# A hybrid S5 / attention / gated-MLP layer on one core: another order of the seven products in the up projection, single PSUM banks in the down projection, and VectorE for the late low parts

## The chip, the cores and the metric

The kernel runs on 1 core of one Trainium2 chip, as one program. The metric is the device time of one execution in microseconds (us), the median of several runs. A profile is one further execution, recorded by the hardware profiler; its span runs from the first to the last instruction.

## The reference

One layer of a diffusion backbone works on 1,024 latent tokens of 1,024 channels, with 256 context tokens beside them. Its first half mixes tokens (a state-space branch and differential attention); the change leaves it alone. Its second half is a gated MLP with a short convolution, and all of the change lies there:

```python
def conv_ffn(h, w_up, conv_w, conv_b, w_down):
    u = h @ w_up
    n = u.shape[1]
    pad = CONV_W // 2
    up = jnp.pad(u, ((0, 0), (pad, pad), (0, 0)))
    y = conv_b
    for j in range(CONV_W):
        y = y + up[:, j:j + n] * conv_w[j]
    a, g = jnp.split(y, 2, axis=-1)
    return (jax.nn.silu(g) * a) @ w_down
...
    x = x + ga1 * merge_branches(g, y_s5, y_attn, p['b_gate'], p['w_out'])
    x = x + ga2 * conv_ffn(modulate(x, p['norm2_w'], sh2, sc2), p['w_up'], p['conv_w'], p['conv_b'], p['w_down'])
```

D_FF is 2816 = 22 x 128, so `w_up` has 44 blocks of 128 columns: 22 for `a` and 22 for `g`.

## The kernel before

**Data.** Activations lie transposed: 128 channels on the partitions, 1,024 tokens along the free axis, in two halves `t0` and `t1` of 512. Each operand of a matmul is split in a high part (`copy` to fp32r, by ScalarE) and a low part (source minus high part, by VectorE or GpSimd); a product is high x high, high x low and low x high, three matmuls for each block of 128 input channels. One PSUM bank holds 128 x 512 fp32 values.

**The up projection** makes, for each hidden block f of 22, the two tiles `va` (the `a` rows) and `ga` (the `g` rows), 128 x 1,024 each, in two banks each. Weights (two blocks of output rows, two halves `lo` and `hi` of the input channels) and activations (two halves of the channels, two halves of the tokens) make a 2 x 2 by 2 x 2 block product, done with seven products instead of eight (Winograd's form of Strassen's algorithm). The activations' factors, `B11`, `B21`, `T1`, `T2`, `B22`, `T3`, `T4`, are made once, at the *seam* before f = 0, by `modulate0` and `modulate1`; `factor` makes high and low part of one block. The weights' factors are made for each f: `up_open` splits the `a` weights, `sums` makes S1 to S4 by four additions, and `piece` splits each. The gate's raw half `A22` is a factor as it is.

For each f, `up_open` runs two products of 12 matmuls: `lo` x B11 into a single bank (`bank()`, 2 buffers `z`), copied out as p1, and `hi` x B21 into `va`'s lower half (`banks()`, 3 buffers `up` of two banks). `up_close` runs the other five products: S1 x T1 (upper half of `ga`), S2 x T2, S4 x B22 (upper half of `va`), S3 x T3 (single bank) and A22 x T4 (lower half of `ga`), with VectorE's sums between them. The sums are u2 (product S2 x T2 plus p1), p1 again (upper `ga` plus u2), u3 (product S3 x T3 plus u2), and one that completes each half of `va` and `ga`. Then `gated` convolves both tiles (`conv`: one pass by ScalarE, four by VectorE, straight from PSUM), applies SiLU and multiplies; the result goes to memory (`Fd`) until the down projection.

**The down projection** sums over the 22 hidden blocks in five parts. For each part and each output block m of 8, both halves of the tokens have a gemm of 3 x (blocks of the part) matmuls into a bank, and VectorE adds the bank, scaled, to `x1[m]` (L1664). For even m the two halves take two single banks `z`, for odd m one tile `up` of two banks. `parted` splits the hidden blocks, by VectorE for the first part and by GpSimd for the rest; GpSimd also makes the low parts of all `w_down` blocks.

**Order.** TensorE's instructions stand as the program writes them (`manual_schedule`). The queues of VectorE, ScalarE, GpSimd and the DMA queue of SyncE are ordered when the program is built, by a scheduler; each engine runs its queue in order and waits on semaphores. Waits are set by whole tiles: an instruction that writes one half of a tile waits for all earlier readers and writers of that tile on other engines.

## Time and profile before

| | before |
|---|---|
| median of 3 runs | 2249.25 us (2249.17 to 2251.09) |
| the profiled execution, its own time | 2250.89 us |
| its span | 2249.1 us |
| mean granted clock of TensorE | 0.961 of full |
| TensorE matmul busy | 2061.7 us, 92% of the span |
| VectorE busy | 1358.4 us, 60% |
| GpSimd busy | 926.4 us, 41% |
| ScalarE busy | 843.4 us, 37% |
| first product of the up projection | 1399.90 us after the start |
| first matmul of the down projection | 1973.23 us |

Engines are named PE (TensorE), DVE (VectorE), ACT (ScalarE), POOL (GpSimd) and SP (SyncE). The granted clock is the share of TensorE's full 2.4 GHz that the chip let through; its two levels are 1.2 and 2.4 GHz, so a mean between 0.5 and 1 is a mixture of both. The stretch from 1399.90 us to the end, 849.2 us, holds everything that the change touches.

### The profile page before, as it was taken

The numbers are of one execution on the slowest core, as the hardware profiler recorded it, in microseconds if no ns is written. First come the engines' busy times: TensorE is split into PE (matmuls) and PEld (weight loads), VectorE is DVE, ScalarE is ACT, GpSimd is POOL, SyncE is SP. The second block draws the span as 40 slices with busy tenths as digits, with TensorE's granted clock in tenths as the row PEclk, the third lists the DMA queues.
The fourth block names the chain that finished last, engine by engine and source line by source line (L and its number), as shares of the span: only waits on it lengthen the run. The fifth ranks groups of instructions, "written<-read, shape, count | busy, mean of one in ns | idle before, by whom it ended". The sixth has DMA issues, their size and how long they took to land.

```text
span 2249.1 us, 29026 instructions
## 1 busy us (share of the span) xinstructions
PE 2061.7 (92%) x10392; PEld 1667.0 (74%) x10392; DVE 1358.4 (60%) x2606; ACT 843.4 (37%) x1509; POOL 926.4 (41%) x1016
## 2 busy tenths in 40 slices
PE   7988899989999999999999999588888888889998
PEld 4766688756688879999998777466777677667776
DVE  6988924999830428888885525765555555542211
ACT  4334434122123227888884023433333333331110
POOL 2476401344104513666665556443333333264311
PEclk9999999999999999999999999799899999999999
DMA  8345654455664263223212554022121121343212
GB/s 308 115 103 143 160 172 145 143 156 149 217 219 155 89 220 109 80 85 104 75 50 67 168 182 127 28 94 66 57 69 68 61 66 66 114 141 108 56 46 88
DMA packets 164625, 262.49 MB, mean 117 GB/s; under 512 B 28672, under 2 KB 92544, under 8 KB 164480
## 3 DMA queue, kind: packets, MB, share of 16 engines
q1 hardware_dynamic: 154400, 242.28, 35.1%
q10 hardware_dynamic: 10080, 18.35, 2.2%
q8 instruction: 82, 1.34, 0.3%
q14 instruction: 63, 0.52, 0.1%
HBM read 188.68 MB, written 71.89 MB: 116 GB/s over the span
## 4 chain that ended last, share of the span: by engine, by line
PE 67%; DVE 23%; DMA 4%; issue 3%; ACT 2%; POOL 2%; SPq 0%; DVEq 0%; ACTq 0%; POOLq 0%
PE ta L1040 6%; PE up L1488 4%; PE up L1489 4%; PE up L1490 4%; PE sc L1240 3%; PE sc L1241 3%; PE up L1267 3%; PE z L1269 3%; PE z L1268 3%; PE z L1267 3%; PE up L1268 3%; PE up L1269 3%; DVE y L1685 2%; PE tb L1022 2%; PE z L555 2%
## 5 line engine op out<-in xcount | busy, mean ns | idle before, releaser
L1242 DVE TENSOR_REDUCE mx<-sc 128x1 f32<-128x1280 f32 x128 | 190.8, 1491 | 53.2 <-PE sc L1241 52.3
L597 POOL TENSOR_TENSOR wlo<-wraw,whi 128x1024 fp32r<-128x1024 f32 x40 | 97.6, 2456 | 245.6 <-ACT whi L596 243.6
L418 PE MATMUL z<-whi,hTh 128*128 128x512 f32 x448 | 182.4, 411 | 3.6 <-ACT hTh L407 3.6
L419 PE MATMUL z<-wlo,hTh 128*128 128x512 f32 x448 | 181.2, 405 | 0.3 <-POOL wlo L597 0.3
L420 PE MATMUL z<-whi,hTl 128*128 128x512 f32 x448 | 179.5, 402 | 0.0
L995 ACT ACTIVATE e<-sc,mx 128x1280 f32<-128x1280 f32 x128 | 172.0, 1344 | 12.6 <-DVE mx L1242 10.9
L1040 PE MATMUL ta<-V,at 128*128 128x128 f32 x1280 | 168.1, 275 | 0.7 <-ACT at L1029 0.7
L1040 PEld LDWEIGHTS ta<-V,at 128*128 128x128 f32 x1280 | 155.5, 191 | 1.0 <-ACT at L1029 0.9
L1488 PE MATMUL up<-tt,rh 128*128 128x512 f32 x176 | 88.0, 500 | 74.4 <-DVE up L1556 74.4
L1685 DVE SCALAR_TENSOR_TENSOR y<-up,small,y 128x896 f32<-128x896 f32 (+1 forms) x176 | 123.7, 745 | 53.3 <-ACT y L1680 52.5
L1240 PE MATMUL sc<-K,q 128*128 128x512 f32 (+1 forms) x384 | 147.7, 385 | 0.7 <-ACT e L995 0.7
L1241 PE MATMUL sc<-K,q 128*128 128x512 f32 (+1 forms) x384 | 131.9, 358 | 0.0
L1481 POOL TENSOR_TENSOR pl<-s,ph 128x512 fp32r<-128x512 f32 x44 | 58.8, 1339 | 174.9 <-ACT ph L1480 174.9
L1255 POOL TENSOR_TENSOR wlo<-wraw,whi 128x1024 fp32r<-128x1024 f32 (+1 forms) x36 | 74.9, 2084 | 120.9 <-ACT whi L1254 120.9
L1659 POOL TENSOR_TENSOR wlo<-wraw,whi 128x640 fp32r<-128x640 f32 (+2 forms) x40 | 56.1, 1404 | 161.8 <-ACT whi L1658 160.8
L1488 PEld LDWEIGHTS up<-tt,rh 128*128 128x128 f32 x176 | 42.2, 240 | 93.5 <-DVE up L1556 72.7
L418 PEld LDWEIGHTS z<-whi,hTh 128*128 128x128 f32 x448 | 86.5, 193 | 33.4 <-issue 10.6
L555 PE MATMUL z<-hTh,whi 128*128 128x512 f32 x256 | 102.4, 400 | 0.0
L420 PEld LDWEIGHTS z<-whi,hTl 128*128 128x128 f32 x448 | 86.9, 194 | 19.3 <-issue 1.0
L557 PE MATMUL z<-hTh,wlo 128*128 128x512 f32 x256 | 100.6, 394 | 0.0
L556 PE MATMUL z<-hTl,whi 128*128 128x512 f32 x256 | 100.2, 393 | 0.0
L1013 DVE SCALAR_TENSOR_TENSOR e<-e,r,e 128x1280 f32<-128x1280 f32 x64 | 99.3, 1552 | 1.1
(497 smaller groups left out, 5736.2 us busy)
## 6 DMA issues: line engine op xcount, KB each, us to landing
wraw<-in_wup_dram SPq DMA_DIRECT2D x46, 512.0 KB
wraw<-in_win_dram SPq DMA_DIRECT2D x44, 512.0 KB
araw<-in_ada_dram SPq DMA_DIRECT2D x32, 512.0 KB
q<-Qd SPq DMA_DIRECT2D x128, 128.0 KB
Kd<-st SPq DMA_DIRECT2D x80, 128.0 KB
K<-Kd SPq DMA_DIRECT2D x16, 640.0 KB
Fd<-y SPq DMA_DIRECT2D x20, 512.0 KB
graw<-Fd SPq DMA_DIRECT2D x20, 512.0 KB
```

Of the source, the lines that this page charges most:

```text
L418: nc.tensor.matmul(pz, hh, wh, start=k == 0, stop=False)
L419: nc.tensor.matmul(pz, hh, wl, start=False, stop=False)
L420: nc.tensor.matmul(pz, hl, wh, start=False, stop=k == KT - 1)
L555: nc.tensor.matmul(pz, wh, hTh[k][:, tok], start=k == 0, stop=False)
L995: nc.scalar.activation(em, S[i]["sc"][m][:, :LK], AF.Exp, bias=S[i]["mx"][:, m:m + 1], accum_out=S[i]["l1"] if m else S[i]["l0"])
L1040: nc.tensor.matmul(PO[p][:, j * P:j * P + P], AT[p, kt // 2][:, kt % 2, j * P:j * P + P], W[:, kt], start=kt == 0, stop=kt == NKT - 1)
L1240: nc.tensor.matmul(sc[:, a:b], Q[0][:, m, qs], K[m][:, a:b], start=True, stop=False)
L1241: nc.tensor.matmul(sc[:, a:b], Q[1][:, m, qs], K[m][:, a:b], start=False, stop=True)
L1242: nc.vector.tensor_reduce(S["mx"][:, m:m + 1], sc[:, :LK], axis=AX.X, op=OP.max, negate=True)
L1267: mm(o, W[0][:, k], ah[k], start=k == 0, stop=False)
L1488: mm(o, W[0][:, k], bh[k], start=k == 0, stop=False)
L1685: stt(y[:, o], pu[:, i], ww, y[:, o], op0=OP.mult, op1=OP.add)
```

## The change

The five products of `up_close` stand in another order, A22 x T4 ahead of S3 x T3. The two sums that end `ga` become one over both halves, with u3 broadcast. To go with that, `sums` and `up_close` make the pieces in the order S4, A22, S3, and `modulate1` makes T4 ahead of T3. All low parts of `factor` are VectorE's, where GpSimd made every second one of T1 and T2, and for f = 0 VectorE makes the low parts of the three late pieces. The down projection gets a PSUM pool of its own, `psD`, with eight single banks, opened once the last block's convolution is issued; that `gated` call now stands ahead of the splits of the first two blocks.

```diff
--- before.py
+++ after.py
@@ -1420,12 +1420,12 @@
             spare += [w[:, 0], w[:, 1]]
         spare = iter(spare)
 
-        def factor(name, k, src, e):
+        def factor(name, k, src):
             if k == 0:
                 B[name] = ([], [])
             h, l = next(spare), next(spare)
             nc.scalar.copy(h, src)
-            e.tensor_tensor(l, src, r32(h), op=OP.subtract)
+            nc.vector.tensor_tensor(l, src, r32(h), op=OP.subtract)
             B[name][0].append(h)
             B[name][1].append(l)
 
@@ -1456,29 +1456,28 @@
             pz = spread(1)
             tt = nc.vector.tensor_tensor
             t0, t1 = halves
-            v, g = nc.vector, nc.gpsimd
             for k in range(KH):
                 b12 = scaled(k, 1, pz)
                 tt(x1[k][:, t0], b12, x1[k][:, t0], op=OP.subtract)
-                factor("T1", k, x1[k][:, t0], v if k % 2 else g)
+                factor("T1", k, x1[k][:, t0])
             for k in range(KH):
                 b22 = scaled(k + KH, 1, pz)
                 tt(x1[k][:, t0], b22, x1[k][:, t0], op=OP.subtract)
-                factor("T2", k, x1[k][:, t0], v if k % 2 else g)
+                factor("T2", k, x1[k][:, t0])
             for k in range(KH):
-                factor("B22", k, x1[k + KH][:, t1], v)
+                factor("B22", k, x1[k + KH][:, t1])
+            for k in range(KH):
+                tt(x1[k + KH][:, t0], x1[k + KH][:, t0], x1[k][:, t0], op=OP.subtract)
+                factor("T4", k, x1[k + KH][:, t0])
+            for k in range(KH):
                 tt(x1[k][:, t1], x1[k + KH][:, t1], x1[k][:, t1], op=OP.subtract)
-                tt(x1[k + KH][:, t0], x1[k + KH][:, t0], x1[k][:, t0], op=OP.subtract)
-            for k in range(KH):
-                factor("T3", k, x1[k][:, t1], v)
-            for k in range(KH):
-                factor("T4", k, x1[k + KH][:, t0], v)
-
-        def piece(pool, src, tag, bufs):
+                factor("T3", k, x1[k][:, t1])
+
+        def piece(pool, src, tag, bufs, e=nc.gpsimd):
             h = self.t(pool, [P, KH, P], tag + "h", bufs, F32R)
             l = self.t(pool, [P, KH, P], tag + "l", bufs, F32R)
             nc.scalar.copy(h, src)
-            nc.gpsimd.tensor_tensor(l, src, r32(h), op=OP.subtract)
+            e.tensor_tensor(l, src, r32(h), op=OP.subtract)
             return h, l
 
         def product(o, W, name):
@@ -1531,14 +1530,14 @@
             tt(a, ra[:, hi], b, op=OP.subtract)
             b = s()
             tt(b, ra[:, lo], rg[:, lo], op=OP.subtract)
-            S["rest"] = a, b, rg[:, hi]
+            S["rest"] = a, rg[:, hi], b
 
         def up_close(fp, f):
 
             p1, va = opened.pop(f)
             t0, t1 = halves
             tt = nc.vector.tensor_tensor
-            S["S4"], S["S3"], S["A22"] = (piece(fp, x, "r", 3) for x in S["rest"])
+            S["S4"], S["A22"], S["S3"] = (piece(fp, x, "r", 3, nc.gpsimd if f else nc.vector) for x in S["rest"])
             tt(va[:, t0], va[:, t0], p1, op=OP.add)
             ga = banks()
             product(ga[:, t1], S["S1"], "T1")
@@ -1549,13 +1548,13 @@
             tt(p1, ga[:, t1], u2, op=OP.add)
             product(va[:, t1], S["S4"], "B22")
             tt(va[:, t1], va[:, t1], p1, op=OP.add)
+            product(ga[:, t0], S["A22"], "T4")
             pz = bank()
             product(pz, S["S3"], "T3")
             u3 = self.t(fp, [P, 512], "q3", 1)
             tt(u3, pz, u2, op=OP.add)
-            tt(ga[:, t1], ga[:, t1], u3, op=OP.add)
-            product(ga[:, t0], S["A22"], "T4")
-            tt(ga[:, t0], ga[:, t0], u3, op=OP.add)
+            g2 = ga.rearrange("p (h n) -> p h n", h=2)
+            tt(g2, g2, u3[:, None].to_broadcast([P, 2, 512]), op=OP.add)
             return va, ga
 
         def gated(fp, f, va, ga):
@@ -1637,10 +1636,12 @@
                 e.tensor_tensor(l, g, r32(h), op=OP.subtract)
                 return h, l
 
+            raws[NF - 1] = gated(fp, NF - 1, *rows)
+            ps_st.close()
+            pd_, pd_st = self.pool("psD", space=PSUM)
             pre = {f: parted(f, nc.vector) for f in (0, 1)}
             for k in range(KT):
                 nc.sync.dma_start(x1[k], X1d[k])
-            raws[NF - 1] = gated(fp, NF - 1, *rows)
             for part, fs in enumerate(parts):
                 last = part == len(parts) - 1
                 gts = [pre[f] if f in pre else parted(f, nc.gpsimd if part else nc.vector) for f in fs]
@@ -1657,9 +1658,8 @@
                     W = [self.t(self.fw, [P, KT, P], x, 3, F32R)[:, :n] for x in ("whi", "wlo")]
                     nc.scalar.copy(W[0], rw)
                     nc.gpsimd.tensor_tensor(W[1], rw, r32(W[0]), op=OP.subtract)
-                    pu = banks() if m % 2 else None
                     for tok in halves:
-                        pd = bank() if pu is None else pu[:, tok]
+                        pd = self.t(pd_, [P, 512], "d", 8)
                         self.gemm(pd, W, [x[0][:, tok] for x in gts], [x[1][:, tok] for x in gts])
                         nc.vector.scalar_tensor_tensor(x1[m][:, tok], pd, self.modT[:, 40 + m, 0:1], x1[m][:, tok],
                                                        op0=OP.mult, op1=OP.add)
@@ -1668,7 +1668,7 @@
         dp_st.close()
         fp_st.close()
         self.fw_st.close()
-        ps_st.close()
+        pd_st.close()
 
     def conv(self, fp, pu, ft):
 
```

How the change moves instructions, at three places.

First, TensorE in the up projection, the block f = 3, as in every later one. `z` is a single bank, `up` a tile of two, `rh` and `rl` are a weight piece's two parts; before, `tt_2863` to `tt_2866` are T3 and `tt_2867` to `tt_2870` T4; a bracket names the semaphores that the instruction waits for. Before, the end of S3 x T3 and the start of A22 x T4:

```order
L1488 MATMUL z_14770<-tt_2866_13408,rh_14719 128x512
L1489 MATMUL z_14770<-tt_2866_13408,rh_14719 128x512
L1490 MATMUL z_14770<-tt_2866_13408,rl_14720 128x512
L1488 MATMUL up_14728<-tt_2867_13409,rh_14723 128x512 [waits DVE_49]
L1489 MATMUL up_14728<-tt_2867_13409,rh_14723 128x512
L1490 MATMUL up_14728<-tt_2867_13409,rl_14724 128x512 [waits Pool_49]
```

A22 x T4 is the last product and waits for VectorE. Now (`tt_2863` to `tt_2866` are T4, `tt_2867` on is T3), the end of S4 x B22 and the start of A22 x T4:

```order
L1487 MATMUL up_14667<-tt_2862_13404,rh_14712 128x512
L1488 MATMUL up_14667<-tt_2862_13404,rh_14712 128x512
L1489 MATMUL up_14667<-tt_2862_13404,rl_14713 128x512
L1487 MATMUL up_14725<-tt_2863_13405,rh_14716 128x512 [waits DVE_49,Activation_49]
L1488 MATMUL up_14725<-tt_2863_13405,rh_14716 128x512
L1489 MATMUL up_14725<-tt_2863_13405,rl_14717 128x512 [waits Pool_49]
```

A22 x T4 has moved up by one product, from behind S3 x T3 to behind S4 x B22. It still waits for VectorE: p1's sum reads the upper half of its tile. Then, in the same block, the end of A22 x T4 and the start of S3 x T3, still now:

```order
L1487 MATMUL up_14725<-tt_2866_13408,rh_14716 128x512
L1488 MATMUL up_14725<-tt_2866_13408,rh_14716 128x512
L1489 MATMUL up_14725<-tt_2866_13408,rl_14717 128x512
L1487 MATMUL z_14779<-tt_2867_13409,rh_14720 128x512 [waits Activation_49]
L1488 MATMUL z_14779<-tt_2867_13409,rh_14720 128x512
L1489 MATMUL z_14779<-tt_2867_13409,rl_14721 128x512 [waits Pool_49]
```

S3 x T3 has become the last product; it writes a single bank and waits for its piece alone.

VectorE's queue in the same block, before, from the third sum of weights to the second of `ga`'s two sums (`s` is a sum of weights, `q` are p1, u2 and u3, `y` the convolution):

```order
L1531 TENSOR_TENSOR s_14862<-wraw_14814,s_14856 128x512
L1548 TENSOR_TENSOR q_3126_14754<-z_14741,q_3108_14695 128x512
L1549 TENSOR_TENSOR q_3108_14695<-up_14728,q_3126_14754 128x512
L1533 TENSOR_TENSOR s_14864<-wraw_14814,wraw_14848 128x512
L1551 TENSOR_TENSOR up_14670<-up_14670,q_3108_14695 128x512
L1685 SCALAR_TENSOR_TENSOR y_14799<-up_14670,small_73,y_14799 128x896
L1685 SCALAR_TENSOR_TENSOR y_14799<-up_14670,small_73,y_14799 128x127
L1555 TENSOR_TENSOR q_3128_14783<-z_14770,q_3126_14754 128x512
L1685 SCALAR_TENSOR_TENSOR y_14799<-up_14670,small_73,y_14799 128x896
L1685 SCALAR_TENSOR_TENSOR y_14799<-up_14670,small_73,y_14799 128x127
L1556 TENSOR_TENSOR up_14728<-up_14728,q_3128_14783 128x512
L1558 TENSOR_TENSOR up_14728<-up_14728,q_3128_14783 128x512
```

u3 (L1555) stands between the steps of `va`'s convolution, and `ga`'s two sums are apart. VectorE's queue in that block now:

```order
L1530 TENSOR_TENSOR s_14858<-wraw_14810,s_14852 128x512
L1547 TENSOR_TENSOR q_3126_14751<-z_14738,q_3108_14692 128x512
L1548 TENSOR_TENSOR q_3108_14692<-up_14725,q_3126_14751 128x512
L1532 TENSOR_TENSOR s_14860<-wraw_14810,wraw_14844 128x512
L1550 TENSOR_TENSOR up_14667<-up_14667,q_3108_14692 128x512
L1685 SCALAR_TENSOR_TENSOR y_14795<-up_14667,small_73,y_14795 128x896
L1685 SCALAR_TENSOR_TENSOR y_14795<-up_14667,small_73,y_14795 128x127
L1685 SCALAR_TENSOR_TENSOR y_14795<-up_14667,small_73,y_14795 128x896
L1685 SCALAR_TENSOR_TENSOR y_14795<-up_14667,small_73,y_14795 128x127
L1555 TENSOR_TENSOR q_3128_14792<-z_14779,q_3126_14751 128x512
L1557 TENSOR_TENSOR up_14725<-up_14725,q_3128_14792 128x1024
```

The first five rows stand as they did. Then the convolution of `va` is no longer parted by u3, and one sum of 1,024 columns (L1557) is in the place of L1556 and L1558.

Second, the seam. GpSimd's queue before, with the four low parts of T1 and T2 (`act`) and the three late pieces of f = 0 (`rl`):

```order
L1481 TENSOR_TENSOR pl_14200<-s_14197,ph_14199 128x512
L1428 TENSOR_TENSOR act_1_1_2844_13386<-x_0_2827_13361,act_0_1_2843_13385 128x512
L1428 TENSOR_TENSOR act_5_1_2848_13390<-x_2_2829_13363,act_4_1_2847_13389 128x512
L1428 TENSOR_TENSOR act_1_1_2852_13394<-x_0_2827_13361,act_0_1_2851_13393 128x512
L1428 TENSOR_TENSOR act_5_1_2856_13398<-x_2_2829_13363,act_4_1_2855_13397 128x512
L1481 TENSOR_TENSOR rl_14295<-s_14203,rh_14294 128x512
L1481 TENSOR_TENSOR rl_14299<-s_14205,rh_14298 128x512
L1481 TENSOR_TENSOR rl_14303<-wraw_14189,rh_14302 128x512
L1481 TENSOR_TENSOR pl_14400<-s_14397,ph_14399 128x512
```

Seven of these nine are low parts for the seam.

VectorE's queue now, where the late low parts and the three pieces stand:

```order
L1428 TENSOR_TENSOR act_7_1_2858_13400<-x_3_2830_13364,act_6_1_2857_13399 128x512
L1428 TENSOR_TENSOR tt_2864_13406<-x_5_2832_13366,tt_2864_13406 128x512
L1428 TENSOR_TENSOR tt_2865_13407<-x_6_2833_13367,tt_2865_13407 128x512
L1428 TENSOR_TENSOR tt_2866_13408<-x_7_2834_13368,tt_2866_13408 128x512
L1547 TENSOR_TENSOR q_3047_14333<-z_14320,q_3008_14126 128x512
L1548 TENSOR_TENSOR q_3008_14126<-up_14307,q_3047_14333 128x512
L1480 TENSOR_TENSOR rl_14295<-s_14203,rh_14294 128x512
L1480 TENSOR_TENSOR rl_14299<-wraw_14189,rh_14298 128x512
L1480 TENSOR_TENSOR rl_14303<-s_14205,rh_14302 128x512
L1524 TENSOR_TENSOR s_14396<-wraw_14394 128x512
L1527 TENSOR_TENSOR s_14402<-s_14396,wraw_14392 128x512
L1550 TENSOR_TENSOR up_14101<-up_14101,q_3008_14126 128x512
```

None of the seven is left on GpSimd; the three `rl` stand on VectorE between p1's sum of f = 0 (L1548) and the weight sums of f = 1 (L1524), and the one that completes `va` of f = 0 (L1550) comes after those.

Third, TensorE in the down projection, where the second half of m = 1 starts. Before:

```order
L1267 MATMUL up_17622<-g_3643_17534,whi_17618 128x512
L1268 MATMUL up_17622<-g_3644_17535,whi_17618 128x512
L1269 MATMUL up_17622<-g_3643_17534,wlo_17619 128x512
L1267 MATMUL up_17622<-g_3635_17526,whi_17618 128x512 [waits DVE_49]
L1268 MATMUL up_17622<-g_3636_17527,whi_17618 128x512
L1269 MATMUL up_17622<-g_3635_17526,wlo_17619 128x512
```

The second half's first matmul waits for VectorE. The same place now:

```order
L1267 MATMUL d_17604<-g_3643_17512,whi_17600 128x512
L1268 MATMUL d_17604<-g_3644_17513,whi_17600 128x512
L1269 MATMUL d_17604<-g_3643_17512,wlo_17601 128x512
L1267 MATMUL d_17615<-g_3635_17504,whi_17600 128x512 [waits PE_49]
L1268 MATMUL d_17615<-g_3636_17505,whi_17600 128x512
L1269 MATMUL d_17615<-g_3635_17504,wlo_17601 128x512
```

Before, the second half writes the tile `up_17622` that the first half used and waits for VectorE's reading of it; now it writes another bank, `d_17615`, and waits for no other engine.

## Rows read from the trace of the kernel before

**Rows 1.** Stretches: TensorE, VectorE, ScalarE, GpSimd busy, clock, DMA.

```profile
core 0: us, PE busy (x) PEld busy (x) DVE busy (x) ACT busy (x) POOL busy (x), PEclk, DMA share, GB/s
1350.00:1399.90 49.90, 48.66 (x210) 38.69 (x210) 29.40 (x45) 18.97 (x24) 33.02 (x19) 1.00 0.43 130
1399.90:1504.71 104.81, 73.51 (x263) 55.61 (x262) 73.01 (x116) 43.32 (x63) 49.47 (x26) 0.81 0.18 62
1504.71:1973.23 468.52, 407.75 (x1597) 323.89 (x1596) 262.51 (x376) 155.18 (x190) 160.04 (x111) 0.92 0.21 71
...
1985.12:2249.10 263.98, 244.31 (x1029) 191.87 (x1027) 57.82 (x77) 42.41 (x55) 96.85 (x55) 1.00 0.29 88
```

**Rows 2.** Waits: who for whom; us in total, times, longest.

```profile
PE up L1488 <- DVE up L1556: 74.4, 22, 5.3
...
PE up L1267 <- DVE x1b L1664: 16.0, 19, 0.8
```

**Rows 3.** Timeline, TensorE, f = 3: start, length, instruction, [idle <- releaser].

```profile
1505.57 0.41 PE L1490 MATMUL z<-act,wlo 128*128 128x512 f32 x1
...
1521.51 0.40 PE L1490 MATMUL z<-tt,rl 128*128 128x512 f32 x1
1525.10 0.50 PE L1488 MATMUL up<-tt,rh 128*128 128x512 f32 x1 [3.20 <-DVE up L1556]
```

**Rows 4.** Timeline, VectorE, the same block.

```profile
1512.17 1.22 DVE L1564 TENSOR_TENSOR y<-y,y 128x1024 f32<-128x1024 f32 x1
1515.42 0.69 DVE L1531 TENSOR_TENSOR s<-wraw,s 128x512 f32<-128x512 f32 x1 [2.03 <-POOL pl L1481]
1516.35 0.69 DVE L1548 TENSOR_TENSOR q<-z,q 128x512 f32<-128x512 f32 x1 [0.24 <-PE z L1490]
1517.08 0.69 DVE L1549 TENSOR_TENSOR q<-up,q 128x512 f32<-128x512 f32 x1
...
1519.14 0.70 DVE L1551 TENSOR_TENSOR up<-up,q 128x512 f32<-128x512 f32 x1 [0.31 <-PE up L1490]
...
1522.44 0.68 DVE L1555 TENSOR_TENSOR q<-z,q 128x512 f32<-128x512 f32 x1
...
1524.36 0.69 DVE L1556 TENSOR_TENSOR up<-up,q 128x512 f32<-128x512 f32 x1
```

**Rows 5.** Timeline, GpSimd, the same block.

```profile
1514.10 1.28 POOL L1481 TENSOR_TENSOR pl<-s,ph 128x512 fp32r<-128x512 f32 x1 [7.55 <-ACT ph L1480]
```

**Rows 6.** Seam: timelines of VectorE, GpSimd, TensorE; last row from the chain.

```profile
1413.02 1.88 DVE L1436 TENSOR_TENSOR tmp<-x,z 128x512 f32<-128x512 f32 x3
...
1423.00 1.77 DVE L1428 TENSOR_TENSOR tt<-x,tt 128x512 fp32r<-128x512 f32 x1
...
1428.51 11.83 POOL L1428 TENSOR_TENSOR act<-x,act 128x512 fp32r<-128x512 f32 x1 [4.29 <-ACT act L1427]
...
1440.39 0.80 PE L1489 MATMUL z<-act,ph 128*128 128x512 f32 x1 [4.29 <-POOL act L1428]
...
1444.20 3.50 DMA wraw<-in_wup_dram
```

**Rows 7.** Timeline, TensorE, f = 1: its first and its last product.

```profile
1458.79 0.40 PE L1488 MATMUL up<-act,ph 128*128 128x512 f32 x1
...
1475.16 0.77 PE L1488 MATMUL up<-tt,rh 128*128 128x512 f32 x1 [5.15 <-DVE up L1556]
```

**Rows 8.** Down projection: timeline of TensorE at m = 3; a stretch.

```profile
1993.02 0.39 PE L1269 MATMUL up<-g,wlo 128*128 128x512 f32 x1
1994.26 0.50 PE L1267 MATMUL up<-g,whi 128*128 128x512 f32 x1 [0.84 <-DVE x1b L1664]
...
1985.00:2020.00 35.00, 32.47 (x137) 25.41 (x137) 10.51 (x14) 12.99 (x17) 29.82 (x16) 1.00 0.52 162
```

**Rows 9.** Timeline, start of the down projection: TensorE, VectorE.

```profile
1975.32 0.50 PE L1268 MATMUL z<-g,whi 128*128 128x512 f32 x1 [1.69 <-DVE g L1637]
...
1973.44 0.70 DVE L1558 TENSOR_TENSOR up<-up,q 128x512 f32<-128x512 f32 x1 [4.70 <-PE up L1490]
```

## The prediction, made before the changed kernel was run

> **What bounds the kernel now.** I read the stretches first, then the waits, then single periods in order of time. TensorE is the engine to follow: it is busy 407.75 of the 468.52 us in which hidden blocks f = 3 to 21 are made and 244.31 of the 263.98 us of the down projection, while VectorE, the next, has 262.51 of 468.52 in the first and little in the second [rows 1]. So a gain comes only out of TensorE's own waits and of its clock. The granted clock is the second thing to see: 1.00 (2.4 GHz) before the seam and in the down projection, 0.81 around the seam, 0.92 in the loop [rows 1].
>
> One wait carries the loop: the first matmul of T4's product behind VectorE's L1556, 22 times, 74.4 us [rows 2]. One period shows it: from 1505.57 to 1521.51 there are 69 steps from one matmul to the next, 0.231 us each; then the next matmul starts at 1525.10, 3.59 us later [rows 3]. L1556 (1524.36) adds u3 into the upper half of `ga`; T4's product writes the lower half of the same tile, so it stands until L1556 is through, and L1556 waits for u3, which is behind half of the convolution in VectorE's queue [rows 4]. A period has 84 matmuls, 19.40 us at 0.231; it lasts 468.52 / 19 = 24.66. Of the 5.26 us more, 3.36 are the wait (3.59 less one step of 0.23) and 1.90 are matmuls at the lower level of 1.2 GHz after it, which is what the 0.92 is.
>
> The down projection has a wait of the same kind: at every odd m, the second half's gemm writes the tile whose first half L1664 still reads. It is 0.84 us of idle time by the waits [rows 2], 1.24 from matmul to matmul instead of 0.23 [rows 8], so 1.01 each, and 20 of them (8 m, 5 parts, every second one), at a clock that stays 1.00 [rows 1].
>
> **The change, part by part.** *Order in the loop.* T4's product now comes before T3's, and one sum over both halves ends the block. T4's product no longer waits for u3; it waits for the reader of the upper half that is left, p1's sum (L1549 before, L1548 after). In the period shown that sum starts at 1517.08 and takes 0.69, so it is through at 1517.77 [rows 4]. S4·B22, which stands between, ends its twelve steps at about 1518.9, since L1551 comes right behind it at 1519.14 after 0.31 of waiting for it [rows 4]. So T4's product finds its bank free with about 1.1 us to spare, if p1's sum keeps its place. The last product (T3's) writes a bank of its own. Next are up_open(f + 1), 24 matmuls into other banks, and then S1·T1, which needs `va`'s bank: its convolution has two products and an up_open, 11 us, after L1550. So no product has a reason to wait, and 3.36 goes; and where TensorE had no such waits, in the 49.90 us before the seam (busy 48.66), the clock is 1.00 [rows 1], so I give back the 1.90 as well. Term: 19 × 5.26 = 99.9 us.
>
> *The double sum.* It replaces two of 0.69 and 0.70. VectorE's product of 1,024 columns takes 1.22 [rows 4], two singles 1.40 together; I take 1.25. It is hidden in the loop behind the next up_open (24 × 0.231 = 5.5 us), and VectorE is busy 56% of the loop now [rows 1], about 13.8 us of each period, so 71% of a period of 19.40. Without that cover it would cost its length.
>
> *The seam, f = 0 to 2* (1399.90 to 1504.71, 104.81 us [rows 1]). Before, GpSimd makes four low parts of T1 and T2; the last takes 11.83 us and TensorE waits for it until 1440.39 [rows 6]. After, VectorE makes all. In its queue the last low part of T2 is the 41st instruction from 1413.02, and a step there is 0.60 us (three in 1.88 [rows 6]): 1437.7. Six more (three lows of T4, u2, p1, S4's low) end at 1441.5, so S4·B22 can go on about 2 us sooner than now. The seven moved low parts (four factors, three pieces) are not free: they lie on this queue, and that is why it is only 2. Then f = 1: its S1·T1 needs `va` of f = 0 out of its bank, so L1550, its copy by ScalarE and four convolution steps must be through. L1550 stands behind L1524, which waits for a load; the load is issued when A22's low is made (1442.1), lands 3.50 later [rows 6], so L1550 runs at about 1447.0 and S1·T1 starts at about 1453.4, against 1458.79 [rows 7]. T4's product of f = 1 then waits for p1's sum, which stands behind u3, the double sum, a load and the convolution: about 1464, and T3's another 3.5 to 4 later, so f = 1 ends near 1470.5. Before, its last product starts at 1475.16 after a wait of 5.15 [rows 7] and ends near 1479.4. With a wait of 1 to 1.5 left in f = 2, I put f = 3 at 1492.7: term 12 us, an estimate from these rows. Its ends are 8 (two more conflicts and a slow stretch) and 15 (VectorE at 0.60 throughout, no slow stretch).
>
> *The start of the down projection.* TensorE now stands until 1975.32 for the low part of block 0, because L1558 (0.70) is ahead of it on VectorE [rows 9]. After, u3 (0.68 [rows 4]) and the double sum (1.25) are ahead of it: 1.2 us worse. Moving `gated` ahead of the split changes nothing in VectorE's order there.
>
> *Single banks.* Every second-half gemm gets a bank of its own out of eight, and L1664, one pass over 512 columns, has seven gemms of at least 2.1 us (9 matmuls) to read it. Term 20 × 1.01 = 20.2. What is late next is GpSimd, which is busy 29.82 of 35.00 us at the start of the projection (splits of blocks and of weights [rows 8]) while TensorE now asks for its weights sooner: I take 1 us off, between 0 and 4. Closing the old PSUM pool makes the first gemms wait for readers of `va` and `ga` of f = 21; eight banks in turn give each of them time, and I take nothing; at most it is a convolution's four steps, some 3 us, within the range.
>
> **Sum.** 99.9 + 12 + 20.2 - 1.2 - 1 = 129.9 us off the profiled span of 2249.1: 2119.2. The median is 2249.25, 0.15 above that span (the profiled execution's own time was 2250.89), so I predict 2119 us.
>
> **Rivals.** *A short wait stays in every period.* The margin of T4's product is 1.1 us. p1's sum stands behind L1530, which waits for GpSimd (2.03 and then 0.24 idle in the row pair [rows 4]; GpSimd's part there takes 1.28 [rows 5]). A low part by VectorE, 0.60 as a step, took 1.77 at 1423.00, in the stretch where GpSimd makes its own [rows 6]. The Trainium skill (GPSIMD Engine Reference, Specifications) says the same in general: GpSimd's SBUF interfaces are shared with VectorE, and collide with VectorE instructions that read two SBUF inputs. The trace agrees, with 1.77 against 0.60, and it speaks against this order, in which GpSimd's low part of S3 now runs after the weight split and so closer to VectorE's next sums. One such conflict of 1.1 eats the margin; beyond it each 0.5 to 1.5 us costs 10 to 28: 2129 to 2147, mid 2138. Against it: in the period shown VectorE idles 2.03 before L1531.
>
> *The short waits also keep the clock low.* Rows against it: waits of 0.84 at clock 1.00 [rows 1, 2]. It would be 2119 + 19 × (1 + 1.9) = 2174. The Trainium skill (TensorE: Matmul & The Clock Gate, A second HAM failure mode: psum-queue depth-cycling) has short idles between groups of matmuls making the clock swing; the down projection of this trace does not show that.
>
> *The waits go and the clock does not come back:* 2119 + 19 × 1.9 = 2155.
>
> *The wait only moves* (T4's product waits for a late p1 as long as it did for u3): the loop gives nothing, 2249 - 30 = 2219.
>
> *Slower: GpSimd is starved in every period.* The 11.83 us part [rows 6] shows how long GpSimd's subtraction can be held while VectorE runs without a gap. L1530 waits for such a part and p1's sum is behind it. If that happened in each block, p1 would come 10.55 later; less 1.1 of margin and 0.24, T4 would wait 9.2 and lose 1.9 of clock, 5.8 more than now: 2249 + 19 × 5.8 - 30 = 2329. It decides once the wait in each block passes 5 us. Against it: no row of the loop has it, and VectorE's gaps stay.
>
> **Numbers.** Forecast 0.65, with 2112 to 2127 as its own range; the seam at 15 and nothing lost to GpSimd, 0.06, 2113; short waits 0.15, with the clock 0.03; clock not back 0.07; wait moved 0.02; slower 0.02. From 2111 to 2140 lie the first two and over half of the third, some 0.8. Only the last is slower, and a measurement of this kernel tells 0.2% (4.5 us) from nothing; so faster 0.97, same 0.01, slower 0.02.
>
> **What would show it.** Right: T4's matmuls without a wait from f = 3, blocks 19.4 us apart at clock 1.00, one VectorE sum of 1,024 columns near 1.25, no GpSimd subtraction in the seam before f = 1, no wait of L1267 for L1664. Wrong: a wait of T4 for p1's sum in steady blocks, a granted clock near 0.9 in the loop, TensorE waiting for GpSimd's weight splits for more than 4 us in all, or a VectorE sum far above 1.4.

## The result and the profile after

The changed kernel takes 2121.24 us (median of 4 runs, 2117.70 to 2125.45) beside 2250.17 us of the kernel before on the same chip (4 runs). The ratio is 0.9427, with a 95% interval from 0.9405 to 0.9448. The forecast was 2119, in a range from 2111 to 2140. The profiled execution took 2117.70 us, the fastest of the four, with a span of 2115.9.

Stretches of the changed kernel, with the columns of [rows 1]: the seam from the first product to f = 3, the loop of f = 3 to 21, the down projection after its first waits.

```profile
1399.10:1492.62 93.52, 73.39 (x263) 53.80 (x262) 76.40 (x119) 42.73 (x62) 27.56 (x19) 0.82 0.20 69
1492.62:1861.30 368.68, 368.68 (x1597) 300.34 (x1596) 264.86 (x357) 153.04 (x190) 169.92 (x112) 1.00 0.26 89
1864.60:2115.90 251.30, 247.45 (x1055) 199.57 (x1055) 65.93 (x87) 44.87 (x58) 97.91 (x56) 0.99 0.31 97
```

The second row is the main reading: TensorE is busy for the whole of the 368.68 us and its clock is 1.00, where [rows 1] have 407.75 busy of 468.52 at 0.92. So 99.84 us are gone there, 11.29 in the seam (104.81 to 93.52) and 21.27 in the down projection (275.87, from 1973.23 to the end, to 254.60). The first product starts 0.80 sooner.

All waits of TensorE from 1390 to the end, with the columns of [rows 2]:

```profile
PE z L1488 <- DVE act L1428: 6.1, 4, 4.4
PE up L1487 <- DVE q L1548: 3.7, 1, 3.7
PE up L1487 <- ACT act L1427: 3.5, 1, 3.5
PE d L1268 <- DVE g L1636: 3.1, 2, 2.9
PE up L1488 <- DVE act L1428: 3.0, 4, 1.9
PE up L1487 <- DVE y L1685: 2.1, 1, 2.1
PE up L1489 <- DVE rl L1480: 1.7, 1, 1.7
```

Both rows of [rows 2] are gone, the 22 waits for `ga`'s sum and the 19 for `x1b`. None of the seven lies in f = 3 to 21. One steady block shows how near the next one is. VectorE, then GpSimd, then the first matmul of A22 x T4:

```profile
1619.94 0.69 DVE L1530 TENSOR_TENSOR s<-wraw,s 128x512 f32<-128x512 f32 x1 [1.18 <-POOL pl L1480]
1620.55 0.68 DVE L1547 TENSOR_TENSOR q<-z,q 128x512 f32<-128x512 f32 x1
1621.26 0.69 DVE L1548 TENSOR_TENSOR q<-up,q 128x512 f32<-128x512 f32 x1
```

```profile
1618.08 1.82 POOL L1480 TENSOR_TENSOR pl<-s,ph 128x512 fp32r<-128x512 f32 x1 [6.21 <-ACT ph L1479]
```

```profile
1622.84 0.39 PE L1487 MATMUL up<-tt,rh 128*128 128x512 f32 x1
```

p1's sum (L1548) ends at 1621.95, and the product that waits for it starts at 1622.84: 0.89 us to spare. GpSimd's low part took 1.82 where [rows 5] have 1.28, L1530 waited for it, and u2 and p1 came behind. Over the 19 blocks of this profile the spare time runs from 0.26 to 1.17, with a median of 1.10.

The start of the down projection, and VectorE ahead of it, beside [rows 9]:

```profile
1864.64 0.50 PE L1268 MATMUL d<-g,whi 128*128 128x512 f32 x1 [2.94 <-DVE g L1636]
```

```profile
1861.50 0.69 DVE L1555 TENSOR_TENSOR q<-z,q 128x512 f32<-128x512 f32 x1 [0.76 <-PE z L1489]
1862.23 1.23 DVE L1557 TENSOR_TENSOR up<-up,q 128x1024 f32<-128x1024 f32 x1
1863.37 2.35 DVE L1636 TENSOR_TENSOR g<-graw,g 128x1024 fp32r<-128x1024 f32 x2
```

u3 and the double sum (1.23 us) stand ahead of the split, and the wait is 2.94 where it was 1.69.

### The profile page after: what moved, and what is told of

Same layout as the page of the kernel before. It is cut to its first block, busy times and chain, and to the rows that moved or that the text cites. A ratio compares the mean times of both kernels' runs of the same rounds, so it can differ in the third digit from the quotient of the medians.

```text
span 2115.9 us, 29038 instructions
## 1 busy us (share of the span) xinstructions
PE 2016.6 (95%) x10392; PEld 1643.8 (78%) x10392; DVE 1364.6 (64%) x2591; ACT 840.7 (40%) x1509; POOL 915.0 (43%) x1009
## 4 chain that ended last, share of the span: by engine, by line
PE 70%; DVE 21%; DMA 4%; issue 3%; POOL 1%; ACT 1%; SPq 0%; DVEq 0%; ACTq 0%; POOLq 0%
PE ta L1040 7%; PE d L1268 4%; PE d L1269 4%; PE d L1267 4%; PE up L1488 4%; PE up L1489 4%; PE up L1487 4%; PE sc L1240 3%; PE sc L1241 3%; PE z L1487 3%; PE z L1489 3%; PE z L1488 3%; PE tb L1022 3%; DVE X L939 2%; DVE sc L936 2%
## 5 line engine op out<-in xcount | busy, mean ns | idle before, releaser
L1664 DVE SCALAR_TENSOR_TENSOR x1b<-d,modT,x1b 128x512 f32<-128x512 f32 x80 | 59.8, 750 | 181.3 <-PE d L1269 181.3
L1480 POOL TENSOR_TENSOR pl<-s,ph 128x512 fp32r<-128x512 f32 x44 | 65.0, 1479 | 182.5 <-ACT ph L1479 182.5
L1268 PE MATMUL d<-g,whi 128*128 128x512 f32 x352 | 139.8, 397 | 3.1 <-DVE g L1636 3.1
L1267 PE MATMUL d<-g,whi 128*128 128x512 f32 x352 | 139.5, 396 | 0.0
L1269 PE MATMUL d<-g,wlo 128*128 128x512 f32 x352 | 139.3, 396 | 0.0
L419 PEld LDWEIGHTS z<-wlo,hTh 128*128 128x128 f32 x448 | 87.5, 195 | 17.4 <-POOL wlo L597 0.7
```

What stands on the lines that cost most here:

```text
L419: nc.tensor.matmul(pz, hh, wl, start=False, stop=False)
L1267: mm(o, W[0][:, k], ah[k], start=k == 0, stop=False)
L1268: mm(o, W[0][:, k], al[k], start=False, stop=False)
L1269: mm(o, W[1][:, k], ah[k], start=False, stop=k == n - 1)
```

## The experiments

Twelve more runs were made; e9 is the changed kernel again and e10 is e5 again. Stages of the profiled executions, in us, and the medians. "One block" is the loop divided by 19; its 84 matmuls take 19.40 at 0.231:

| kernel | seam to f = 3 | loop f = 3 to 21 | one block | down projection | span | median |
|---|---|---|---|---|---|---|
| before | 104.81 | 468.52 | 24.66 | 275.87 | 2249.1 | 2250.17 |
| changed | 93.52 | 368.68 | 19.40 | 254.60 | 2115.9 | 2121.24 |
| e1, loop part alone | 91.76 | 370.10 | 19.48 | 276.3 | 2137.0 | 2139.73 |
| e2, banks alone | 105.64 | 468.46 | 24.66 | 253.8 | 2226.3 | 2230.35 |
| e3, seam alone | 105.24 | 469.02 | 24.69 | 274.8 | 2247.3 | 2249.04 |
| e4, one sum moved | 88.84 | 368.60 | 19.40 | 276.3 | 2132.9 | 2133.53 |
| e5, e4 with banks | 88.94 | 368.66 | 19.40 | 256.5 | 2111.9 | 2113.70 |
| e6, seam given back | 91.85 | 372.77 | 19.62 | 255.3 | 2119.8 | 2119.27 |
| e7, u2 three times | 99.69 | 402.75 | 21.20 | 254.7 | 2157.4 | 2159.16 (1 run) |
| e8, u2 five times | 102.77 | 448.77 | 23.62 | 256.4 | 2210.0 | 2211.74 (1 run) |
| e9, changed again | 95.33 | 370.23 | 19.49 | 254.6 | 2118.8 | 2121.92 |
| e10, e5 again | 87.26 | 368.66 | 19.40 | 255.0 | 2108.8 | 2112.89 |
| e11, u2 eight times | 108.54 | 501.79 | 26.41 | 255.5 | 2266.7 | 2268.49 (1 run) |
| e12, two single sums | 92.43 | 368.76 | 19.41 | 256.7 | 2120.4 | 2122.18 (1 run) |

**e1, e2 and e3: each part of the change alone, on the kernel before.** e1 takes the order of the products, of the pieces and of T4 and T3, and the double sum:

```diff
-            S["S4"], S["S3"], S["A22"] = (piece(fp, x, "r", 3) for x in S["rest"])
+            S["S4"], S["A22"], S["S3"] = (piece(fp, x, "r", 3) for x in S["rest"])
...
+            product(ga[:, t0], S["A22"], "T4")
             pz = bank()
             product(pz, S["S3"], "T3")
...
-            tt(ga[:, t1], ga[:, t1], u3, op=OP.add)
-            product(ga[:, t0], S["A22"], "T4")
-            tt(ga[:, t0], ga[:, t0], u3, op=OP.add)
+            g2 = ga.rearrange("p (h n) -> p h n", h=2)
+            tt(g2, g2, u3[:, None].to_broadcast([P, 2, 512]), op=OP.add)
```

> The kernel before with the loop's part of the change alone: T4's product ahead of T3's, one double sum, pieces and factors in that order; GpSimd keeps its low parts at the seam, the down projection keeps its paired banks. Theory 1 (T4's product stood behind the sum of u3 into the other half of its tile; that wait and the slow clock after it are the gain): blocks f = 3 to 21 fall from 24.66 to 19.4 us each, 100 us, and the waits of 5.2 in f = 0 and 1 go too, some 8 of the 11 us that the seam gave; about 2141. Rival (the late low parts by VectorE are what gave the seam's gain): the loop's 100 and nothing at the seam, 2150.

e2 takes the single banks of the down projection, with their pool and the earlier place of the last `gated`, which the cut leaves out:

```diff
-                    pu = banks() if m % 2 else None
...
-                        pd = bank() if pu is None else pu[:, tok]
+                        pd = self.t(pd_, [P, 512], "d", 8)
```

> The kernel before with the single banks of the down projection alone. Theory 1: the 20 waits for L1664 go, 1.0 to 1.1 us each, 20 to 22 us off: 2229. Rival (GpSimd's splits are late next and take half of it back): TensorE waits for the low parts of weights in the first part, 2238 to 2240.

e3 lets VectorE make the seam's low parts:

```diff
-                factor("T1", k, x1[k][:, t0], v if k % 2 else g)
+                factor("T1", k, x1[k][:, t0], v)
...
-                factor("T2", k, x1[k][:, t0], v if k % 2 else g)
+                factor("T2", k, x1[k][:, t0], v)
...
-            S["S4"], S["S3"], S["A22"] = (piece(fp, x, "r", 3) for x in S["rest"])
+            S["S4"], S["S3"], S["A22"] = (piece(fp, x, "r", 3, nc.gpsimd if f else nc.vector) for x in S["rest"])
```

> The kernel before with the seam's engines alone: all late low parts and the three pieces of f = 0 by VectorE, order and banks as before. Theory 1: the 11.83 us part of GpSimd goes, VectorE's own queue takes its place, and S4 x B22 of f = 0 starts about 2 us sooner: 2 to 4 us off, 2247. Rival: the part of GpSimd was the seam's cost, 8 to 11 us off, 2240.

e1's ratio is 0.9510 (0.9496 to 0.9525), e2's 0.9909 (0.9894 to 0.9924), e3's 0.9992 (0.9983 to 1.0002), all to 2251.13 us of the kernel before. The loop part brings 98.4 us in the loop and 13.05 in the seam by itself, the banks 22.0 in the down projection, and VectorE's taking over nothing that can be told from noise. What happened to it shows in five rows of e3, TensorE and then VectorE, with one of TensorE in the kernel before at the end:

```profile
1434.33 0.79 PE L1489 MATMUL z<-act,ph 128*128 128x512 f32 x1 [0.76 <-DVE act L1428]
1439.87 0.79 PE L1490 MATMUL up<-tt,rl 128*128 128x512 f32 x1 [1.66 <-DVE rl L1481]
1452.96 0.77 PE L1488 MATMUL up<-tt,rh 128*128 128x512 f32 x1 [6.38 <-ACT rh L1480]
```

```profile
1444.59 0.69 DVE L1525 TENSOR_TENSOR s<-wraw 128x512 f32<-128x512 f32 x1 [3.57 <-DMA wraw<-in_wup_dram]
1452.13 0.69 DVE L1556 TENSOR_TENSOR up<-up,q 128x512 f32<-128x512 f32 x1
```

```profile
1443.54 0.63 PE L1490 MATMUL up<-tt,rl 128*128 128x512 f32 x1
```

The matmul of S2 x T2 that stood until 1440.39 [rows 6] goes on at 1434.33; measured from each kernel's first product (1399.90 and 1398.23) that is 4.4 us sooner. S4 x B22 then waits 1.66 us for its piece's low part and goes on at 1439.87, where the kernel before had come at 1443.54: 2.0 us sooner by the same measure. But A22 x T4 of f = 0 starts 54.73 us after the first product, against 54.48 before. The trace names ScalarE's `rh` as what it waited for, but that piece was made 15 us earlier; what ended just ahead of the product is L1556, at 1452.82, and that stands behind a weight load. So the work became earlier and the wait took it all back.

**e4: only one sum moves.** The products keep their order:

```diff
-            tt(ga[:, t1], ga[:, t1], u3, op=OP.add)
             product(ga[:, t0], S["A22"], "T4")
+            tt(ga[:, t1], ga[:, t1], u3, op=OP.add)
             tt(ga[:, t0], ga[:, t0], u3, op=OP.add)
```

> The kernel before with one line moved: u3's sum into the upper half of the tile is written behind T4's product instead of ahead of it; the products keep their order, T4's last. Theory 1 (a wait for a reader and writer of the same tile, nothing else): T4's product then waits for p1's sum alone, two products earlier, so the loop gives the same 100 us as in the loop-only kernel, 2141 to 2145. Rival (the order of the products itself is worth something): blocks stay clearly above 19.4 us, and the time lies above 2160.

The ratio is 0.9481 (0.9462 to 0.9500), and each block is 19.40. The loop as one stretch, with the columns of [rows 1], has no idle time:

```profile
1488.05:1856.65 368.60, 368.60 (x1597) 300.45 (x1596) 266.15 (x378) 155.32 (x191) 163.36 (x112) 1.00 0.26 89
```

So the whole gain of the loop comes from one instruction that no longer stands between two products on the same tile; the other order of the products adds nothing to it. The time is 7.5 us below the range that I expected. In the seam e4 is 2.9 us ahead of e1.

**e5 and e10: e4's moved line with e2's banks**, the same program on two chips, the second time in turns with the changed kernel.

> The kernel before with the one moved line and the single banks, nothing else: the products stay in their old order, GpSimd keeps its low parts at the seam, the two sums stay single. If the terms add up, 2133.5 less the 22 of the banks, 2111 to 2113, some 8 below the changed kernel. Rival, the terms are not independent, because the start of the down projection waits for the sums behind T4's product and for the readers of the banks: 2118 or more.

> The kernel before with the one moved sum and the single banks, beside the changed kernel on the same chip. From the runs so far: 2111 to 2115, 6 to 9 below the changed kernel's median. Here T4's product stands last and p1's sum has the whole of S3's product to come, so no block has a wait of T4's product. Rival, the lead is a difference between chips: within 2 us of the changed kernel.

e5: 2113.70 us (2109.79 to 2116.62), ratio 0.9393 (0.9378 to 0.9407). e10: 2112.89 (2110.60 to 2114.67), ratio 0.9392 (0.9379 to 0.9404), where the changed kernel beside it (e9) has 2121.92 (2119.19 to 2124.88) and 0.9429 (0.9414 to 0.9443). The two terms add up, and this kernel is the fastest of all, by 9 us. The spans differ by 10.0: 8.07 in the seam, 1.57 in the loop and 0.77 before the first product, less 0.4 in the down projection.

**e6: the changed kernel with GpSimd's low parts at the seam given back** (the reverse of e3's edit).

> The changed kernel with GpSimd's low parts at the seam given back to it. If VectorE's taking them over is worth 2 to 3 us, the stretch from the first product to f = 3 grows from 93.5 to 96. Rival, by the kernel with the loop part alone (91.8): it shrinks to 92 and the time is 2 us below the changed kernel's.

The seam is 91.85, as the rival said, though the time is within the spread of the changed kernel's (2119.27, 2116.36 to 2124.93). And T4's product waits in three blocks of its loop. VectorE in the block before such a wait (first four rows) and in one with it, then GpSimd in the latter, then TensorE:

```profile
1748.32 2.85 DVE L1685 SCALAR_TENSOR_TENSOR y<-up,small,y 128x896 f32<-128x896 f32 x4
...
1754.76 0.69 DVE L1530 TENSOR_TENSOR s<-wraw,s 128x512 f32<-128x512 f32 x1 [1.18 <-POOL pl L1480]
1755.37 0.68 DVE L1547 TENSOR_TENSOR q<-z,q 128x512 f32<-128x512 f32 x1
1756.08 0.69 DVE L1548 TENSOR_TENSOR q<-up,q 128x512 f32<-128x512 f32 x1
...
1767.28 0.69 DVE L1524 TENSOR_TENSOR s<-wraw 128x512 f32<-128x512 f32 x1 [1.75 <-DMA wraw<-in_wup_dram]
...
1768.67 2.85 DVE L1685 SCALAR_TENSOR_TENSOR y<-up,small,y 128x896 f32<-128x896 f32 x4
...
1775.12 1.83 DVE L1530 TENSOR_TENSOR s<-wraw,s 128x512 f32<-128x512 f32 x1 [1.19 <-POOL pl L1480]
1776.88 0.68 DVE L1547 TENSOR_TENSOR q<-z,q 128x512 f32<-128x512 f32 x1
1777.59 0.69 DVE L1548 TENSOR_TENSOR q<-up,q 128x512 f32<-128x512 f32 x1
```

```profile
1773.26 3.15 POOL L1480 TENSOR_TENSOR pl<-s,ph 128x512 fp32r<-128x512 f32 x2 [7.06 <-ACT ph L1479]
```

```profile
1778.43 0.47 PE L1487 MATMUL up<-tt,rh 128*128 128x512 f32 x1 [1.07 <-DVE q L1548]
```

A load landed late, so VectorE's convolution stands 20.35 us after the one before instead of 19.40. L1530 then meets GpSimd's second low part (two in a row, 3.15), takes 1.83 instead of 0.69, and p1's sum comes 21.51 after the one before. That is 2.11 late and more than the margin.

**e9: the changed kernel once more.**

> The changed kernel once more, for its spread. In the trace already seen T4's product never waits from f = 3 on, but in the kernel with GpSimd's seam parts given back it waited in three blocks of nineteen, 1.07 to 1.26 us each, where a weight load landed about 1 us later and VectorE's third weight sum (L1530) fell together with GpSimd's second low part, 1.83 instead of 0.69 us. If that is chance and not a matter of the edit, a second execution of the changed kernel shows such blocks too, each 1.1 to 1.5 us longer, and the median stays at 2121 within 3. Rival, the waits belong to the other kernel alone: none here, and a span within 1 us of 2116.

It has one such block: L1530 took 1.77, T4's product waited 1.29, the block 20.94. Over five profiles with the new order (changed, e1, e6, e9, e12) T4's product waits for p1's sum in 5 blocks of 95; over three with the old one (e4, e5, e10) in none of 57. In four of the five the first weight sum (L1524, in e1 L1525) had waited 1.75 to 2.08 us for its load, and the fifth came straight behind one of them.

**e7, e8 and e11: u2's sum made three, five and eight times** in the changed kernel, which writes the same values again and delays p1 by known steps:

```diff
             tt(u2, pz, p1, op=OP.add)
+            tt(u2, pz, p1, op=OP.add)
+            tt(u2, pz, p1, op=OP.add)
             tt(p1, ga[:, t1], u2, op=OP.add)
```

> The changed kernel with u2's sum made three times in a row in every block (the same values written again), so that p1's sum comes later by two steps of some 0.6 us. The margin of T4's product is 0.8 to 0.9 in the changed kernel's trace. Expected: T4's product waits about 0.5 to 1 us in each block, blocks of 20 to 20.4, clock 1.00 in the loop; about 2130 to 2141. Rival, any wait in each block lowers the clock: blocks near 22, 2170 to 2177.

> The changed kernel with u2's sum made five times in every block: p1's sum comes later by four steps, some 2.4 to 3 us, so T4's product waits about 1.6 to 2.2 us in each block. Blocks of 21 to 21.6 if the clock stays at 1.00, 2152 to 2164; 23 to 23.4 if it falls after each wait as it did after the waits of 3.2 us before, 2190 to 2198.

> The changed kernel with u2's sum made eight times in every block (the same values written again): p1's sum comes 7 steps of some 0.6 us later, 1.9 more than with five sums, so T4's product waits about 4 us in each block. If it is the length of one wait that takes the clock down, the clock falls after every wait: blocks of 19.4 + 4.1 + 1.9 = 25.4, the loop's granted clock near 0.92 as in the kernel before, and about 2236. Rival, only every third or fourth block loses the clock, as with waits of 2.2: blocks near 24.1, clock 0.95 to 0.97, about 2212.

The loop's waits and stretches, e7, e8 and e11 in turn:

```profile
PE up L1487 <- DVE q L1550: 26.4, 19, 3.1
```

```profile
PE up L1487 <- DVE q L1552: 52.8, 19, 5.2
```

```profile
PE up L1487 <- DVE q L1555: 89.0, 19, 6.9
```

```profile
1499.95:1902.70 402.75, 376.32 (x1598) 301.22 (x1596) 287.74 (x395) 150.01 (x190) 172.48 (x113) 0.99 0.24 82
```

```profile
1504.86:1953.63 448.77, 396.01 (x1597) 315.33 (x1596) 318.25 (x434) 150.69 (x190) 165.86 (x111) 0.94 0.22 74
```

```profile
1509.40:2011.19 501.79, 412.83 (x1598) 328.24 (x1596) 356.08 (x490) 152.96 (x190) 165.88 (x111) 0.89 0.20 66
```

A mean wait of 1.39 us (26.4 / 19) makes a block 1.80 longer, one of 2.78 makes it 4.22, one of 4.68 makes it 7.01; before, the idle time of 3.20 by the same view made it 5.26. (The prediction's 3.36 is the same wait, taken from matmul to matmul.) What is beyond the wait is 0.41, 1.44, 2.33 and 2.06. All three kernels are slower than I expected: an added sum took 0.72 us and not 0.6, a weight sum (L1532) came to stand ahead of p1's, and the seam grew too, to 99.69, 102.77 and 108.54.

The rival of e7, a clock that falls after any wait, is wrong: after its 16 waits of 0.73 to 1.42 in the loop none of the next 39 matmuls is slow (a slow one is 0.43 us from the next, where the others are 0.23). In e8 five waits of 2.18 in the loop had no slow matmul behind them either. But two others of 2.18 and every one from 2.21 on were followed by 7 to 10. Two waits of e8, with and without, and the 12 us from each on, with the clock in the third column from the end:

```profile
1568.65 0.47 PE L1487 MATMUL up<-tt,rh 128*128 128x512 f32 x1 [2.18 <-DVE q L1552]
1592.07 0.47 PE L1487 MATMUL up<-tt,rh 128*128 128x512 f32 x1 [2.18 <-DVE q L1552]
1568.65:1580.65 12.00, 11.99 (x45) 9.62 (x46) 7.70 (x10) 5.08 (x6) 4.92 (x3) 0.86 0.21 66
1592.07:1604.07 12.00, 12.00 (x52) 9.75 (x53) 7.32 (x10) 4.96 (x6) 4.96 (x3) 1.00 0.22 71
```

In e11 the clock falls after every wait, as expected. Outside the loop the length of the wait does not settle it either: at the start of the down projection slow matmuls followed a wait of 2.94 in the changed kernel, in e6 and in e11, and none followed one of 2.94 or 2.95 in e1, e8 and e9.

**e12: two single sums** in place of the double one, in the changed kernel:

```diff
-            g2 = ga.rearrange("p (h n) -> p h n", h=2)
-            tt(g2, g2, u3[:, None].to_broadcast([P, 2, 512]), op=OP.add)
+            tt(ga[:, t1], ga[:, t1], u3, op=OP.add)
+            tt(ga[:, t0], ga[:, t0], u3, op=OP.add)
```

> The changed kernel with two single sums at the end of ga in place of the double one. By my step the double sum is hidden behind the next up_open: blocks stay 19.4, the start of the down projection moves by 0.1 to 0.2, and the time is the changed kernel's within its own spread. Rival, the order of T4 and S3 needs the double sum, because single sums of 0.69 come apart in VectorE's queue and push the next block's weight sums: blocks of 20 or more, 2130 or above.

Blocks of 19.41 and a time within the changed kernel's spread: the double sum is worth nothing that can be seen here. The wait at the start of the down projection is 3.15, against 2.94 with it.

## Why the prediction was right, and where it was not

**The loop: right, cause shown.** The term was 99.9 and it measures 99.84. Both halves of it came: 3.36 of waiting, and 1.90 because the clock went back to 1.00. e4 gets the same by moving one line, so the wait for L1556 was the cause of both. e8 and e11, which put long waits back, bring the slow matmuls back with them; e7, with short ones, brings the waits alone in 17 of 19 blocks.

**The margin: right in the middle, its spread missed, and my rival half seen.** The median of 1.10 is the 1.1 worked out, but single blocks have as little as 0.26, and five blocks of e1, e6 and e9 less than nothing. The mechanism of *A short wait stays* is real: L1530 at 1.83 for 0.69 while GpSimd subtracts, p1's sum behind it. The Trainium skill (GPSIMD Engine Reference, Specifications) has GpSimd's SBUF interfaces shared with VectorE, and contention with VectorE instructions that have two SBUF inputs; L1530 is one, and e6's rows agree. But it makes the product wait in some blocks and not in every one, and costs 1.3 to 1.6 us a time. That a load that lands late sets it off is read from the rows of e1, e6 and e9; it was not tried by itself. *The short waits also keep the clock low* is refuted for waits up to 1.42 by e7. The Trainium skill (TensorE: Matmul & The Clock Gate, A second HAM failure mode: psum-queue depth-cycling) has frequent short idles between groups of matmuls making the clock swing; e7's waits of up to 1.42 us do not show that, while the waits from 2.21 us on in e8's loop agree with it.

**The seam: the size right by luck, the argued cause wrong.** 11.29 us against 12, and f = 3 starts at 1492.62 where I had 1492.7. But the step that failed is "S4·B22 can go on about 2 us sooner than now" as a reason for gain. VectorE's taking over does bring these 2.0 us, and e3 shows that it ends nothing sooner: alone it is worth -0.4 us in the stretch. e6 without it is 1.7 faster there than the changed kernel, which is no more than two profiles of the changed kernel differ (93.52 and 95.33). The loop's edit carries the seam's whole gain (e1, 13.05): three of the waits for L1556 lie in f = 0 to 2 (5.26, 5.15 and 3.20 us), and in e1 they are gone for one of 4.12 for p1's sum. That f = 3 came within 0.1 us is luck, because f = 1 ended at 1473.16 where I had 1470.5, and f = 2 had no wait and took 19.46 where I had left 22.2. My other two steps came nearly as worked out: S1 x T1 of f = 1 started at 1453.69 (1453.4 predicted), and T4's product of that block at 1465.96 (1464), after this wait:

```profile
1465.96 0.47 PE L1487 MATMUL up<-tt,rh 128*128 128x512 f32 x1 [3.73 <-DVE q L1548]
```

That wait is what the new order costs: p1's sum is needed one product sooner, in a block in which VectorE is late. The old order has twelve more matmuls between, and in e10 the same product of f = 1 starts without a wait:

```profile
1460.70 0.68 DVE L1549 TENSOR_TENSOR q<-up,q 128x512 f32<-128x512 f32 x1
```

```profile
1462.93 0.39 PE L1488 MATMUL up<-tt,rh 128*128 128x512 f32 x1
```

From S1 x T1 of f = 1 to f = 2 e10 takes 13.92 us (1451.80 to 1465.72), the changed kernel 19.47 (1453.69 to 1473.16). That is 5.55 of the 6.26 us between their seams. Why VectorE's queue reaches p1's sum so much later in the changed kernel, where a weight sum of f = 2 took 2.19 us after a wait of 2.38 for its load, was not tried by itself.

**The down projection: mechanism right, 3 us too small.** By the steps from matmul to matmul the 20 waits were 20.5 us (20.2 worked out), and the start is 1.25 worse, against 1.2. What I left out is the matmul behind each wait: it takes 0.50 at its start and the next follows 0.33 later, not 0.23, as before at 1994.26 [rows 8] and then here:

```profile
1994.59 0.39 PE L1268 MATMUL up<-g,whi 128*128 128x512 f32 x1
```

Twenty of these are 2 us. The 1 us for GpSimd did not come in the profile of the changed kernel: TensorE waits for no weight split there. In the other nine runs with single banks it waits 0.17 to 1.70 in all, so that bound was of the right order.

**The sum.** 99.84 + 11.29 + 21.27 + 0.80 are the 133.2 us between the spans, 2249.1 to 2115.9. The prediction had 129.9. The median lies 5.3 above the profiled span because other executions were slower than that one; e9's late block and longer seam (95.33) show two ways how.

## What to carry to other kernels

Where waits are set by whole tiles, a sum on one half of a PSUM tile holds up the product into the other half; move the sum behind the product before touching the order of the products. A stall of 3 us on TensorE cost 5, because the clock fell after it, while stalls of 0.73 to 1.42 us made their blocks 0.98 to 1.64 longer (e7). When an edit makes one input earlier, look for the wait that ends last behind it: here VectorE took seven subtractions from GpSimd, S4 x B22 came 2.0 us sooner, and the next wait took them back.

## What was not expected of the hardware

- Over all profiles, no wait of up to 1.70 us that TensorE reached at full clock in the up projection had slow matmuls behind it. Between 1.85 (f = 2 of e9, with) and 2.95 us (e9 at the start of the down projection, without) some had them and some not, and from 3.06 us on all had. I had expected all or nothing.
- A VectorE sum with two SBUF inputs (L1530) and a GpSimd subtraction hold each other up, and the one that starts second pays. In e6 (above) GpSimd's second low part started 0.01 us ahead of L1530 and took its 1.29, while L1530 took 1.83. In e12 L1530 started 0.05 us ahead, kept its 0.69, and GpSimd's part took 1.81:

```profile
1661.89 0.69 DVE L1530 TENSOR_TENSOR s<-wraw,s 128x512 f32<-128x512 f32 x1 [1.19 <-POOL pl L1480]
1661.94 1.81 POOL L1480 TENSOR_TENSOR pl<-s,ph 128x512 fp32r<-128x512 f32 x1
```

In all fourteen profiles this sum (L1531 in the kernels that are made from the one before) is longer than 0.70 only where a GpSimd subtraction began before it. So offsets of less than 0.1 us decide, and the same program has blocks of 19.40 and of 20.7 to 21.0.
